# The order of the work at the start of a two-layer diffusion trunk: the second half of x loaded and normed before two of the four modulation chunks, more sums left open, and products of constants on TensorE

## The chip, the cores and the metric

The kernel runs on one core of a Trainium2 chip. The metric is device time in microseconds (us) of one execution, the median of three runs. 0.2% of it is 4.65 us.

TensorE (PE) multiplies into PSUM, which has eight banks; its weight loads (PEld) run beside its products. VectorE (DVE), ScalarE (ACT) and GpSimd (POOL) do the elementwise work, and SyncE's queue (SP) issues all transfers. Each engine takes its instructions in the order in which they stand, and waits on semaphores of the others.

## The reference, cut to what matters

Two layers, each for 128 context tokens and 512 latent tokens (640 in all, D = 1024). What the start of a layer computes:

```
mod = silu(cond) @ w_ada + b_ada
shift, scale, gate = split(mod, 3)
h = rms_norm(x, norm_g) * (1 + scale) + shift
z = h @ w_in
```

`cond` is one vector for the context tokens and one for the latents. After this come four mixers on parts of z (RWKV, latent attention, gMLP, FNet), gated merging, and x + gate * (merged @ w_out). The outputs are the normed x, the final RWKV states and the attention caches of the context.

## The kernel before, in words

All is kept with features on the partitions: x is 8 tiles of 128 features by 640 tokens, and the tokens are worked on in two halves of 320 (`HALVES`). A product of a float32 matrix with h is done as three products of rounded parts: a number is split into hi and lo (`split`, L143: hi on ScalarE, L144; lo on GpSimd, or on VectorE where the caller says V, L145), and `dense_half` (L161) adds hi*hi, hi*lo and lo*hi for each k of 8, lines 168 to 170, into one bank of PSUM. One column block of z for one half is thus 24 products of 320 columns.

The start of layer 0 stands in `layer` (L340), in the branch `l == 0`. Its parts, each a generator that can be run in steps:

- `load_x` (L304) issues 8 transfers of one half of x, 160 KB each.
- `norm_first` (L308): the squares on ScalarE and their sum on VectorE (L274, L276), `token_rstd` (L278) with two products with ones on PE (L280, L281), a reciprocal root with a Newton step (L186 to L193), then x times it, six tiles on VectorE and two on GpSimd (L316).
- `ada` (L236): the modulation in chunks of 512 outputs. Chunk 0 and 1 are the shift, 2 and 3 the scale; chunks 0 and 2 serve the features of k = 0 to 3, chunks 1 and 3 those of k = 4 to 7. They come in the order 0, 2, 1, 3. A chunk takes six steps: 4 transfers of 512 KB (`ar`); the products of its first four k; those of the other four (L249); the copy of the sum on ScalarE (L253); a step without work; four small products that turn the row into columns and add the bias (L258, L260).
- `tiles` (L319): `norm_scale` makes s = (1 + scale) * norm_g on VectorE (L291), and `norm_tile` (L294) makes h for one k: hi on ScalarE (L300), the same on VectorE (L301), and lo as the difference (L302), on VectorE for even k and on GpSimd for odd.
- `weights(i, k)` (L1187) loads and splits four k (256 KB) of the weights of column block 13 + i; `chunk(i, q)` (L1184) is that block for one half. Its four steps have two k each; the result is copied by ScalarE (L1185).

In the names of the profile, hhi and hlo are h's parts, wh and wl those of block 13, w10h to w30l those of blocks 14 to 16 for k = 0 to 3, and w14h to w34l for k = 4 to 7. m is a small sum in PSUM, dps a sum of `dense_half`.

Inside `tc.manual_schedule()` the instructions stand on each engine as the program is written; behind it a scheduler of the framework sets the order. Before the change: norm of the first half, chunk 0, weights, chunk 2, tiles 0 to 3 of the first half; then the four blocks' first parts (k = 0 to 3) are put between the steps of chunks 1 and 3, so that the blocks' sums stay open; then the weights of k = 4 to 7, x's second half is loaded, tiles 4 to 7 are made, and the open sums are finished while the second half is normed. Last, all four blocks of the second half.

PSUM is shared out by `banks` (L71): in this part four banks for sums of `dense_half` (`d`) and four for small sums (`m`, taken in turn by `bank1`, L78). The same place in layer 1 isn't touched.

Of the kernel before, what the change touches and what calls it, by code (L numbers as in the profile page):

```python
# [56 lines left out]
def trunk(ctx: ExitStack, tc: tile.TileContext, A: dict, O: dict, dbg: dict):  # L57
    nc = tc.nc
    mm = nc.tensor.matmul
# [280 lines left out]
    def layer(l, X, h, w13):  # L340
# [835 lines left out]
        with ExitStack() as es:  # L1176
# [4 lines left out]
            with tc.tile_pool(name=f"first{l}", bufs=1, side="right") as fp:  # L1181
# [14 lines left out]
                if l == 0:  # L1196


                    with tc.manual_schedule():
                        mod0 = ada(0, (0, 2, 1, 3), 8)  # L1200
                        w = [[], [], [], []]
                        run(norm_first(h, X, HALVES[0]))
                        run(steps(mod0, 6))
                        for i in range(3):
                            weights(i, 0, V)
                        run(steps(mod0, 6))
                        weights(3, 0)
                        weights(0, 4)
                        run(tiles(h, X, 0, HALVES[0]))
                        ahead = [chunk(i, HALVES[0]) for i in range(4)]  # L1210
                        run(steps(ahead[0], 2))
                        run(steps(mod0, 4))
                        run(steps(ahead[1], 2))
                        run(steps(mod0, 2))
                        run(steps(ahead[2], 2))
                        run(steps(mod0, 4))
                        run(steps(ahead[3], 1))
                        run(mod0)
                        run(steps(ahead[3], 1))
                        for i in range(1, 4):  # L1220
                            weights(i, 4)
                        load_x(X, HALVES[1])
                        nc.sync.dma_start(rope, A["rope"])
                        nc.sync.dma_start(fng, A["fng"])
                        run(tiles(h, X, 4, HALVES[0]))
                        second = seq(norm_first(h, X, HALVES[1]), tiles(h, X, 0, HALVES[1]), tiles(h, X, 4, HALVES[1]))
                        run(steps(second, 8))
                        run(ahead[0])
                        run(ahead[1])
                        mix(seq(*ahead[2:]), second, 4.0)  # L1230
                        run(second)
# [10 lines left out]
                for i in range(4):  # L1242
                    run(chunk(i, HALVES[1]))
# [131 lines left out]
    psum_l.enter_context(banks(4, 4))  # L1375
    X = new_x("x0")
# [171 lines left out]
```

## Time and profile before

| what | value |
|---|---|
| median of 3 runs | 2323.45 us (2320.99 to 2325.73) |
| profiled execution | 2330.01 us |
| span of its instructions | 2328.1 us |
| mean granted TensorE clock | 0.980 of 2.4 GHz |
| PE busy | 2183.5 us (94%) |
| DVE, ACT, POOL busy | 1449.2, 1098.4, 894.4 us |
| moved by DMA | 283.73 MB, mean 122 GB/s |

The span runs from the first to the last instruction; times in the rows are us from its start. Busy time is the union of an engine's instructions; products of PE overlap, so a busy PE need not be at its peak, and the granted clock (PEclk, 1.00 is 2.4 GHz, 0.50 is 1.2 GHz) stands beside it. In a row of a timeline, the bracket tells how long the engine was idle before the instruction, and whose work ended that. The change touches some 90 us at the start of the span; the first product of L199, at 88.64 us, comes behind it on PE.

### The profile page before, as it was taken

To read this page: it belongs to the slowest core of one execution; us is meant where nothing else is said; L and a number is where in the kernel's file an instruction comes from. 1 tells how busy PE (TensorE), PEld (TensorE's weight loads), DVE (VectorE), ACT (ScalarE), POOL (GpSimd) and SP (SyncE) were. 2 spreads that over 40 slices of the span, in tenths; PEclk is the share of its full clock that TensorE was granted. 3 is DMA by queue.
4 is the path that set the end of the run, shared out by engine and by line. 5 is a ranking of instruction groups with operands and counts; after the bars stand their busy time and mean duration, and the time that the engine had idled before them with its cause. 6 is when DMAs were issued, how large, how long until landed. Compare 5 with 4: busy or idle time off the path is not lost. (4 is left out here: it accounts for less than half of the span.)

```text
span 2328.1 us, 49632 instructions
## 1 busy us (share of the span) xinstructions
PE 2183.5 (94%) x19662; PEld 2013.7 (86%) x19662; DVE 1449.2 (62%) x2826; ACT 1098.4 (47%) x2387; POOL 894.4 (38%) x894
## 2 busy tenths in 40 slices
PE   6899998898999999899999999989999999998998
PEld 3788898787888999878998888978888899997997
DVE  4777757888884335822367787578889643367234
ACT  4566755444434334422355676544444343344332
POOL 2322224444433335523552212244444334355452
PEclk8999999999999999999999999999999999998999
DMA  7133336333215425565432323362332254264233
GB/s 262 51 108 95 93 98 194 101 100 100 85 56 177 143 80 179 155 219 203 151 98 87 105 81 99 115 197 86 99 88 70 62 178 152 76 187 147 91 102 106
DMA packets 208009, 283.73 MB, mean 122 GB/s; under 512 B 26912, under 2 KB 119712, under 8 KB 207776
## 3 DMA queue, kind: packets, MB, share of 16 engines
q1 hardware_dynamic: 207776, 280.55, 38.1%
q8 instruction: 155, 2.54, 0.5%
q14 instruction: 78, 0.64, 0.1%
HBM read 224.75 MB, written 55.74 MB: 120 GB/s over the span
## 5 line engine op out<-in xcount | busy, mean ns | idle before, releaser
L145 POOL TENSOR_TENSOR wl<-wr,wh 128x512 fp32r<-128x512 f32 x371 | 523.0, 1413 | 975.0 <-ACT wh L144 853.4
L168 PE MATMUL dps<-hhi,wh 128*128 128x320 f32 x2368 | 772.6, 326 | 10.8 <-DVE f L1146 4.2
L169 PE MATMUL dps<-hlo,wh 128*128 128x320 f32 x2368 | 744.7, 314 | 7.9 <-POOL hlo L302 4.5
L170 PE MATMUL dps<-hhi,wl 128*128 128x320 f32 x2368 | 742.2, 313 | 0.0
L168 PEld LDWEIGHTS dps<-hhi,wh 128*128 128x128 f32 x2368 | 452.7, 191 | 25.6 <-ACT hhi L300 4.8
L169 PEld LDWEIGHTS dps<-hlo,wh 128*128 128x128 f32 x2368 | 453.3, 191 | 14.6 <-POOL hlo L302 7.1
L170 PEld LDWEIGHTS dps<-hhi,wl 128*128 128x128 f32 x2368 | 452.1, 191 | 0.5
L144 ACT CAST wh<-wr 128x512 fp32r<-128x512 f32 x372 | 229.6, 620 | 311.0 <-PE dps L169 200.2
L168 PE MATMUL dps<-ohi,wh 128*128 128x320 f32 x512 | 161.6, 316 | 2.1 <-ACT wh L144 1.9
L170 PE MATMUL dps<-ohi,wl 128*128 128x320 f32 x512 | 158.7, 311 | 1.0 <-POOL wl L145 1.0
L822 DVE TENSOR_TENSOR XZ<-XZ,m 128x512 f16<-128x512 f16 x200 | 129.5, 677 | 47.4 <-PE m L819 47.3
L169 PE MATMUL dps<-olo,wh 128*128 128x320 f32 x512 | 159.0, 311 | 0.0
L1146 DVE SCALAR_TENSOR_TENSOR f<-f,dps 128x320 f32<-128x320 f32 x96 | 46.3, 486 | 169.3 <-PE dps L170 169.3
L769 POOL TENSOR_TENSOR GG<-GG,con 64x256 f32<-64x256 f32 x80 | 60.8, 760 | 163.8 <-DVE GG L764 160.6
L1140 ACT ACTIVATE f<-dps,der 128x320 f32<-128x320 f32 x128 | 67.2, 525 | 111.4 <-PE dps L170 104.1
L168 PEld LDWEIGHTS dps<-ohi,wh 128*128 128x128 f32 x512 | 97.0, 189 | 10.6 <-issue 5.9
L170 PEld LDWEIGHTS dps<-ohi,wl 128*128 128x128 f32 x512 | 96.6, 189 | 2.4 <-POOL wl L145 1.5
L169 PEld LDWEIGHTS dps<-olo,wh 128*128 128x128 f32 x512 | 96.9, 189 | 1.7 <-issue 1.7
L812 DVE TENSOR_TENSOR T<-m,con 128x256 f16<-128x256 f32 x200 | 80.7, 416 | 18.6 <-PE m L811 18.0
L774 ACT CAST A<-GG 64x256 f16<-64x256 f32 x80 | 32.3, 403 | 90.4 <-POOL GG L769 90.3
L615 DVE TENSOR_TENSOR pl<-m,ph 128x512 fp32r<-128x512 f32 (+1 forms) x96 | 59.1, 620 | 24.8 <-ACT ph L614 23.5
L818 PE MATMUL m<-T,XZ 128*128 128x64 f16 x800 | 66.0, 195 | 5.2 <-DVE T L812 5.2
(493 smaller groups left out, 4624.4 us busy)
## 6 DMA issues: line engine op xcount, KB each, us to landing
wr<-in_w_in SPq DMA_DIRECT2D x180, 256.0 KB, 2.9
wr<-in_w_merge SPq DMA_DIRECT2D x128, 256.0 KB, 2.7
ar<-in_w_ada SPq DMA_DIRECT2D x48, 512.0 KB, 6.3
wr<-in_w_branch SPq DMA_DIRECT2D x64, 256.0 KB, 2.8
zdr<-f SPq DMA_DIRECT2D x48, 320.0 KB, 3.4
rk<-spill SPq DMA_DIRECT2D x20, 768.0 KB, 5.9
thdr<-t SPq DMA_DIRECT2D x32, 320.0 KB, 3.2
odr<-t SPq DMA_DIRECT2D x32, 320.0 KB, 3.5
```

Of the source, the lines that this page charges most:

```text
L144: S_.copy(hi, src)
L145: (leng or G).tensor_sub(lo, src, hi.bitcast(F32))
L168: mm(ps, hi[:, c], ahi(k)[:, q], start=(k == 0), stop=False)
L169: mm(ps, hi[:, c], alo(k)[:, q], start=False, stop=False)
L170: mm(ps, lo[:, c], ahi(k)[:, q], start=False, stop=(k == K - 1))
L615: V.tensor_sub(pl[:, 0:w], tp[:, 0:w], ph[:, 0:w].bitcast(F32))
L769: G.tensor_sub(GK[HALF[j], j], GK[HALF[j], j], bc(i64[HALF[j]], 4))
L812: V.tensor_mul(T1.rearrange("p u (j k o i) -> p (u j) k o i", j=2, o=2, i=b)[:, :, :, 0, :], ps[:, 0:256].rearrange("p (x k i) -> p x k i" ...
L818: mm(ps[:, 64 * u:64 * u + 64], X1[:, u, :], cols(T1[:, u, :], 0), start=True, stop=True)
L822: V.tensor_add(new, new, ps.rearrange("p (x n i) -> p x n i", x=2, i=b))
L1140: yield from dense(A["w_merge"][l, m, n], 8, H, lambda q, ps: S_.activation(gt[:, q], ps, AF.Tanh, scale=0.5, bias=bias))
L1146: yield from dense(A["w_branch"][l, n, m], 4, (lambda k: o[k][0], lambda k: o[k][1]), lambda q, ps: V.scalar_tensor_tensor(to[:, q], gt[:, ...
```

## The change

- x's second half is loaded right behind the weights of k = 0 to 3, ahead of the transfers of chunks 1 and 3, and normed before the products of chunk 1.
- The four first parts of the first half follow one another without modulation between them. Then come the norm of the second half, chunk 1, tiles 0 to 3 of the second half, the first parts of blocks 13 and 14 for the second half (`late`), chunk 3, the weights of k = 4 to 7 (blocks 13 and 15 split on GpSimd, 14 and 16 on VectorE), tiles 4 to 7 of the first half, its four sums, tiles 4 to 7 of the second half, and the two late sums. Six sums are open at once, so `banks` gives six to `d` and two to `m`.
- `busy(n)` does n products of a 128x128 tile of ones with itself into a small bank, which nobody reads: 24 at the start, 4 in the middle of chunks 0 and 2, 8 behind each.
- Blocks 13 and 14 of the second half are no longer among the blocks behind the branch.

```diff
--- before.py
+++ after.py
@@ -1196,39 +1196,52 @@
                 if l == 0:
 
 
+                    def busy(n):
+
+                        ps = bank1()
+                        for _ in range(n):
+                            mm(ps[:, 0:128], ones, ones, start=True, stop=True)
+
                     with tc.manual_schedule():
                         mod0 = ada(0, (0, 2, 1, 3), 8)
                         w = [[], [], [], []]
+                        busy(24)
                         run(norm_first(h, X, HALVES[0]))
-                        run(steps(mod0, 6))
-                        for i in range(3):
-                            weights(i, 0, V)
-                        run(steps(mod0, 6))
-                        weights(3, 0)
-                        weights(0, 4)
+                        run(steps(mod0, 2))
+                        busy(4)
+                        run(steps(mod0, 4))
+                        weights(0, 0, V)
+                        busy(8)
+                        run(steps(mod0, 2))
+                        busy(4)
+                        run(steps(mod0, 4))
+                        busy(8)
+                        for i in range(1, 4):
+                            weights(i, 0, None if i == 3 else V)
+                        load_x(X, HALVES[1])
+                        run(steps(mod0, 1))
                         run(tiles(h, X, 0, HALVES[0]))
                         ahead = [chunk(i, HALVES[0]) for i in range(4)]
-                        run(steps(ahead[0], 2))
-                        run(steps(mod0, 4))
-                        run(steps(ahead[1], 2))
-                        run(steps(mod0, 2))
-                        run(steps(ahead[2], 2))
-                        run(steps(mod0, 4))
-                        run(steps(ahead[3], 1))
+                        for i in range(4):
+                            run(steps(ahead[i], 2))
+                        run(norm_first(h, X, HALVES[1]))
+                        run(steps(mod0, 5))
+                        run(steps(mod0, 1))
+                        run(tiles(h, X, 0, HALVES[1]))
+                        late = [chunk(i, HALVES[1]) for i in range(2)]
+                        for i in range(2):
+                            run(steps(late[i], 2))
                         run(mod0)
-                        run(steps(ahead[3], 1))
-                        for i in range(1, 4):
-                            weights(i, 4)
-                        load_x(X, HALVES[1])
+                        for i in range(4):
+                            weights(i, 4, V if i % 2 else None)
                         nc.sync.dma_start(rope, A["rope"])
                         nc.sync.dma_start(fng, A["fng"])
                         run(tiles(h, X, 4, HALVES[0]))
-                        second = seq(norm_first(h, X, HALVES[1]), tiles(h, X, 0, HALVES[1]), tiles(h, X, 4, HALVES[1]))
-                        run(steps(second, 8))
-                        run(ahead[0])
-                        run(ahead[1])
-                        mix(seq(*ahead[2:]), second, 4.0)
-                        run(second)
+                        for i in range(4):
+                            run(ahead[i])
+                        run(tiles(h, X, 4, HALVES[1]))
+                        for i in range(2):
+                            run(late[i])
                 else:
                     w = [w13, [], [], []]
                     second = norm_half(l, h, X, HALVES[1])
@@ -1239,7 +1252,7 @@
                         mix(chunk(i, HALVES[0]), second, 0.75 if i else 0.0)
                     run(second)
                 X["pool"].close()
-                for i in range(4):
+                for i in range(0 if l else 2, 4):
                     run(chunk(i, HALVES[1]))
                 shift(13, z, z13)
             rkv = proj_rkv(kp, z13)
@@ -1372,7 +1385,7 @@
 
 
     psum_l = ctx.enter_context(ExitStack())
-    psum_l.enter_context(banks(4, 4))
+    psum_l.enter_context(banks(6, 2))
     X = new_x("x0")
     h = new_h()
     pre = cst.tile([128, 1], F32, name="pre")
```

How this moves the instructions, at three places. SyncE's queue, from the chunk 0 transfers on; cond, x's first half and the constants stand ahead in both (ar is a piece of w_ada, wr a block of weights):

```order
 L244 DMA ar<-in_w_ada 128x1024 x4
-L149 DMA wr<-in_w_in 128x512 x3
+L149 DMA wr<-in_w_in 128x512
 L244 DMA ar<-in_w_ada 128x1024 x4
-L149 DMA wr<-in_w_in 128x512 x2
-L244 DMA ar<-in_w_ada 128x1024 x8
 L149 DMA wr<-in_w_in 128x512 x3
 L306 DMA x<-in_x 128x320 x8
-L1223 DMA rope<-in_rope 128x512
-L1224 DMA fng<-in_fng 128x8
+L244 DMA ar<-in_w_ada 128x1024 x8
+L149 DMA wr<-in_w_in 128x512 x4
```

One weight block instead of three stands ahead of chunk 2, and x's second half has passed the eight transfers of chunks 1 and 3.

VectorE, between the norm of x's first half and its first tile; before (the first mod is chunk 0, the second chunk 2):

```order
L260 TENSOR_TENSOR mod<-m_216,vec 128x8
L145 TENSOR_TENSOR wl<-wr,wh 128x512
L145 TENSOR_TENSOR w10l<-wr,w10h 128x512
L145 TENSOR_TENSOR w20l<-wr,w20h 128x512
L260 TENSOR_TENSOR mod<-m_259,vec 128x8
L291 SCALAR_TENSOR_TENSOR s_277<-mod,vec 128x8
L301 TENSOR_SCALAR t<-x,s_277,mod 128x128
```

and now:

```order
L260 TENSOR_TENSOR mod<-m_246,vec 128x8
L145 TENSOR_TENSOR wl<-wr,wh 128x512
L260 TENSOR_TENSOR mod<-m_291,vec 128x8
L145 TENSOR_TENSOR w10l<-wr,w10h 128x512
L145 TENSOR_TENSOR w20l<-wr,w20h 128x512
L291 SCALAR_TENSOR_TENSOR s_340<-mod,vec 128x8
L301 TENSOR_SCALAR t<-x,s_340,mod 128x128
```

The subtractions for w10l and w20l stood ahead of chunk 2's mod; now they stand between it and s, which every tile needs.

ScalarE, around the copy of chunk 3's sum (m_375 before, m_523 now); before:

```order
L253 COPY t<-m_324 128x512
L253 COPY t<-m_375 128x512
L144 CAST w14h<-wr 128x512
L144 CAST w24h<-wr 128x512
L144 CAST w34h<-wr 128x512
L300 ACTIVATE hhi<-x,mod,s_277 128x128
```

and now, where the first copy is chunk 1's and the four hhi are tiles 0 to 3 of the second half:

```order
L253 COPY t<-m_456 128x512
L300 ACTIVATE hhi<-x,mod,s_340 128x320 x4
L144 CAST uh<-ur 128x128
L253 COPY t<-m_523 128x512
L144 CAST wh<-wr 128x512
L144 CAST w14h<-wr 128x512
L144 CAST w24h<-wr 128x512
L144 CAST w34h<-wr 128x512
L144 CAST uh<-ur 128x128
L300 ACTIVATE hhi<-x,mod,s_340 128x128
```

Chunk 3's copy has four casts of weights behind it, where it had three (the fourth, wh, stood ahead of the first tile), and the tiles of the second half have moved ahead of it.

## Rows read from the trace of the kernel before

**Rows 1.** Stages: us; busy (x) of PE, PEld, DVE, ACT, POOL; PEclk, DMA share, GB/s

```profile
28.92:34.77 5.85, 4.59 (x12) 3.13 (x12) 3.75 (x10) 2.42 (x6) 1.90 (x3) 0.50 1.03 409
34.77:38.19 3.42, 3.42 (x17) 0.60 (x16) 0.00 (x0) 0.00 (x0) 0.00 (x0) 0.53 1.05 373
48.31:55.13 6.82, 3.79 (x13) 2.90 (x14) 6.39 (x13) 5.16 (x13) 3.24 (x4) 0.74 0.45 137
55.13:59.28 4.15, 4.15 (x19) 4.15 (x19) 1.67 (x4) 1.49 (x5) 0.00 (x0) 0.60 0.01 2
59.28:62.90 3.62, 3.62 (x24) 3.30 (x22) 1.74 (x5) 1.21 (x4) 1.76 (x2) 1.00 0.18 65
64.83:76.61 11.78, 8.07 (x38) 6.99 (x39) 9.68 (x16) 5.25 (x11) 8.80 (x8) 0.86 0.08 20
85.12:88.64 3.52, 3.52 (x26) 3.52 (x25) 1.31 (x3) 1.27 (x3) 0.00 (x0) 1.00 0.17 56
```

**Rows 2.** Waits of PE from 0 to 88.64: us in total, times, longest

```profile
PE dps L168 <- ACT hhi L300: 4.2, 3, 1.8
PE dps L169 <- POOL hlo L302: 3.3, 6, 1.2
PE dps L169 <- DVE hlo L302: 2.3, 2, 1.8
```

**Rows 3.** Timeline near 11 us: start, us, engine, line, operation, [idle before <-releaser]

```profile
10.28 1.27 PE L281 MATMUL m<-last,ones 128*128 128x320 f32 x2
...
11.42 0.20 DVE L1384 CAST c<-con 128x64 f16<-128x64 f32 x1 [2.49 <-DMA con<-in_consts]
...
12.26 0.49 DVE L283 TENSOR_SCALAR t<-m 128x320 f32<-128x320 f32 x1
```

**Rows 4.** Timeline from 21 to 30 us

```profile
21.31 0.69 DVE L145 TENSOR_TENSOR w20l<-wr,w20h 128x512 fp32r<-128x512 f32 x1
...
27.37 0.54 DVE L291 SCALAR_TENSOR_TENSOR s<-mod,vec 128x8 f32<-128x8 f32 x1
...
28.92 0.63 PE L168 MATMUL dps<-hhi,wh 128*128 128x320 f32 x1 [1.79 <-ACT hhi L300]
29.58 0.49 DVE L302 TENSOR_TENSOR hlo<-t,hhi 128x320 fp32r<-128x320 f32 x1
```

**Rows 5.** Timeline of PE, first and last product of w14 and of w34

```profile
55.13 0.47 PE L168 MATMUL dps<-hhi,w14h 128*128 128x320 f32 x1
...
58.06 0.47 PE L170 MATMUL dps<-hhi,w14l 128*128 128x320 f32 x1
...
61.24 0.31 PE L168 MATMUL dps<-hhi,w34h 128*128 128x320 f32 x1
...
62.86 0.31 PE L170 MATMUL dps<-hhi,w34l 128*128 128x320 f32 x1
```

**Rows 6.** Timeline of PE, VectorE and GpSimd, norm and tiles of the second half

```profile
59.28 0.70 PE L280 MATMUL m<-acc,ones 128*128 128x320 f32 x2
...
64.83 0.41 PE L168 MATMUL dps<-hhi,wh 128*128 128x320 f32 x1 [1.66 <-ACT hhi L300]
...
70.68 0.97 DVE L302 TENSOR_TENSOR hlo<-t,hhi 128x320 fp32r<-128x320 f32 x1
...
70.36 0.94 POOL L302 TENSOR_TENSOR hlo<-t,hhi 128x320 fp32r<-128x320 f32 x1 [0.85 <-DVE t L301]
```

**Rows 7.** Timeline from 42 to 47 us, chunk 3 of the modulation

```profile
42.82 1.92 PE L249 MATMUL m<-ar,cond 128*32 128x512 f32 x16
...
45.29 0.62 ACT L144 CAST w14h<-wr 128x512 fp32r<-128x512 f32 x1
...
45.81 0.62 ACT L144 CAST w24h<-wr 128x512 fp32r<-128x512 f32 x1
...
46.64 0.17 DVE L260 TENSOR_TENSOR mod<-m,vec 128x8 f32<-128x8 f32 x1 [5.42 <-PE m L258]
...
46.84 0.45 DVE L291 SCALAR_TENSOR_TENSOR s<-mod,vec 128x8 f32<-128x8 f32 x1
```

## The prediction

> **What bounds the kernel now.** The change touches only the start of layer 0, so I read the start. First the table by stage [rows 1]: look at PE's busy time beside the length of the stretch, and at PEclk. From the first product on the normalised x (28.92) to the first product of line 199 (88.64), behind which the order of the work is the same in both kernels, PE has three stretches of work that comes in drops: 28.92 to 34.77, 48.31 to 55.13 and 64.83 to 76.61, in which 12, 13 and 38 products fill 5.85, 6.82 and 11.78 us. Between them are stretches where PE is busy all the time, some at a granted clock of 0.50 to 0.60 of 2.4 GHz. Then the waits of PE in this time [rows 2]: 4.2 us for ScalarE's hhi, 3.3 and 2.3 us for hlo from GpSimd and VectorE. So the norm tiles bound the drops, not the transfers. Ahead of 28.92 PE has only the modulation and the norm's two products to do.
>
> How fast PE can be: twelve products of 320 columns stand 1.62 us from first to last start at full clock (61.24 to 62.86), 2.93 us at half (55.13 to 58.06) [rows 5]. That is 0.147 and 0.266 us each; 12 cost 1.8 or 3.2 us.
>
> **What costs nothing.** The 48 products of 128x128 constants have no row. The nearest are the 128x320 float32 products of L280 and L281, 0.70 us at 59.28 and 1.27 us at 10.28 [rows 3, 6]; by columns 0.28 to 0.51 us each. The first 24 take 6.7 to 12.2 us and may hold L281 back from 10.28 until 13; VectorE then first waits for con until 11.42 and starts L283 at 12.26 [rows 3], and x is wanted only at the first tile, near 28. The groups of four and eight lie between pieces of w_ada that come at 373 GB/s or a little more [rows 1], 1.4 us for 512 KB, and beside ScalarE's and VectorE's steps on the sums; only the last eight can matter (below). With two m banks each new sum waits for the reader of the one but last, long done. Six d banks hold four ahead and two late sums, so no product waits for a bank. On SP's queue, x's second half passes the eight pieces of chunks 1 and 3: 1.3 MB at 409 GB/s [rows 1] puts them back 3.2 us, but they are used only after 41 and 55; the k = 4 weights behind them come near 42 and are used near 58.
>
> **The walk through the new order**, against the same mark at 88.64:
>
> 1. First product. Two weight blocks fewer, 0.52 MB at 0.40 MB/us, stand ahead of chunk 2, so it ends 1.3 us sooner. But on VectorE s (L291) now stands behind w10l and w20l, whose blocks come after chunk 2: 2.0 us for three blocks, then casts 0.5 apart [rows 7] and a subtraction of 0.69 [rows 4]. That puts s near 27.3 as before (27.37), and the product at 28.92 [rows 4]. I take 28.9; ends: 1.3 us sooner, or 1.0 later if the last eight products of constants (8 x 0.51 = 4.1 us, from near 25.8, where chunk 2's small products should end) run at half clock.
> 2. The first four tiles take the 5.85 us of before [rows 1]: to 34.8. At full clock 0.5 less.
> 3. Chunks 1 to 3 now follow at once: 36 products. In this place before, the clock was 0.50 to 0.53 until 38.2 [rows 1]. I take 12 at half clock and 24 at full: 3.2 + 3.5 = 6.7, to 41.5; ends 5.3 and 9.6.
> 4. L280 of the second half stands behind those 36. From L280 to the first product on that half it took 59.28 to 64.83, 5.55 us [rows 6]: to 47.0. Chunk 1's modulation lies inside it (1.92 [rows 7] and its two small steps). No other product is left for PE there.
> 5. Four tiles of the second half: the fourth tile's hlo was done at 71.30 [rows 6], 6.5 us after 64.83; with its two products 7.0, then chunk 1's twelve, 1.8: to 55.8. Ends -1.5 and +1.4.
> 6. Chunk 3 comes only now. 1.92 for its products, then 1.90 to mod (44.74 to 46.64), as before [rows 7]: 59.6. On ScalarE the four casts of the k = 4 weights wait behind the copy of this sum; they end 4 x 0.52 after it, near 60.5; VectorE subtracts w14l and w34l ahead of s. w34l ends near 61.3, and from s to the first product is 1.47 us (46.84 to 48.31 [rows 7, 1]). To 63.0. Before, this link took 48.31 - 44.74 = 3.6 us, now 5.3. Ends -0.7 and +1.9 (chunk 3 at half clock, 3.42 us [rows 1], and the two subtractions beside GpSimd's).
> 7. Tiles 4 to 7 of the first half: 5.85, to 68.9 (6.8 before, when GpSimd still worked on weights; that is the upper end).
> 8. 36 products: 5.3 at full clock, 9.6 at half. I take 5.9, to 74.8.
> 9. The rest: 72 products of the second half, 10.6, and 24 of the next chunk, 3.52 [rows 1]. ScalarE's hhi for tiles 4 to 7 stand behind the copies of the four finished sums, so they start near 75; chunk 2's products run meanwhile and cover most. I take 1.5 us of waiting (0 to 4): 90.4.
>
> So the mark goes from 88.64 to 90.4, **1.8 us later**: the interleaving that is given up (modulation between the open sums) is worth about what x's earlier half brings. The profiled execution took 2330.0 (span 2328.1), so it would take 2331.8; the median shown is 6.6 us below it, which gives 2325.2. I say 2325.
>
> [...] The row: VectorE's hlo took 0.97 us beside GpSimd's 0.94, and 0.49 alone [rows 6, 4], so it is slowed by about the overlap. [...]
>
> **The rivals.** A change within 0.2% of 2323.45 (4.65 us, 2318.8 to 2328.1) is what a measurement of this kernel can't tell from none.
>
> *Faster: every step at its lower end.* The mechanism is the clock: the products of constants hold 2.4 GHz from the start, PE comes out of the first tiles at full clock, L280 is reached sooner, and everything behind it moves up. Steps 1 to 9 then give -1.3, -0.5, -1.4, 0, -1.5, -0.7, 0, -0.6, -1.5: 7.5 us below my sum, 2317.7. For it: the stretch of 34.77 to 38.19 lost half its rate to a clock that fell while PE had little to do [rows 1]. Against it: the new products end near 28, and drops of work that a tile at a time feeds come right after. [...] I give 0.17.
>
> *Slower: the clock falls at the new waits.* Steps 4 to 6 hold 21.5 us with 24 products and two modulation chunks, steps 7 and 9 more drops. In 48.31 to 59.28 a clock that fell among tiles stayed at 0.60 through a busy stretch of 4.15 us [rows 1]. If PE enters step 8 at half clock (+3.7), runs step 5's last twelve so (+1.4) and chunk 3 (+1.5), the mark is 6.6 us later than my sum: 2331.8. It decides at the granted clock near 69. 0.23.
>
> *The change doesn't do what it says.* The products of constants end, the clock is back at 1.2 GHz at the first tile, chunk 2 waits for nothing less: then steps 1 and 3 are at their upper ends (+1.0, +2.9) and the rest as walked, 5.7 us later than before, or 2329 at the worst, while a part of it only gives 2325 to 2328. I count its worst with the slower case.
>
> **How the numbers follow.** My sum and what lies within 4.65 us of before: 0.60. Faster 0.17, slower 0.23. The range 2317.5 to 2331.5 runs from the faster rival to the slower one and leaves out the tails, some 0.2.
>
> **What would show it.** Right: first product on x near 29; no modulation products between it and 41; L280 a second time near 40 to 42; first product on the second half near 45 to 47; chunk 3's products near 54 to 56, and hhi of k = 4 only near 61 to 63, behind w34l; L199 near 90. PE then waits for hhi and hlo about as long as before, in four places instead of three. Wrong: PEclk 1.00 without a gap from 10 to 60 and L199 before 85 (the faster rival), or PEclk 0.5 near 60 to 75 and L199 behind 94 (the slower one), or a wait of PE for DMA in this stretch, which I have at nothing.

## The result, and the profile after

The change is slower. The changed kernel took 2339.56 us (median of 6, 2333.43 to 2340.68), the kernel before, beside it, 2324.59 (2320.99 to 2328.51): ratio 1.006, 95% interval 1.0045 to 1.0074. Two more comparisons gave 1.0047 (1.0034 to 1.0059) and 1.0045 (1.0029 to 1.0061). So it costs 10 to 14 us. I had said 2325.0, between 2317.5 and 2331.5, and had given slower a chance of 0.23.

The profiled execution took 2340.68 us, its span 2337.9, 9.8 more than the span before. The mark, the first product of L199, stands at 93.92 instead of 88.64: 5.3 of the 9.8 arise ahead of it, 4.5 behind it. Stages of the changed kernel up to the mark, cut as steps 2 to 9 of the prediction were (columns as in [rows 1]):

```profile
30.51:35.67 5.16, 3.36 (x13) 2.25 (x13) 4.85 (x11) 4.94 (x13) 1.84 (x2) 0.81 0.97 392
35.67:43.16 7.49, 7.49 (x37) 7.49 (x37) 1.67 (x4) 0.47 (x2) 0.00 (x0) 0.67 0.84 313
43.16:48.34 5.18, 4.15 (x30) 1.96 (x28) 3.20 (x6) 1.71 (x3) 1.13 (x2) 1.00 0.01 3
48.34:55.92 7.58, 4.04 (x13) 3.22 (x14) 6.73 (x18) 1.93 (x4) 3.32 (x4) 0.66 0.00 0
55.92:58.54 2.62, 2.62 (x13) 2.43 (x12) 0.00 (x0) 0.00 (x0) 0.00 (x0) 0.67 0.09 25
58.54:66.61 8.07, 2.98 (x26) 1.39 (x25) 3.93 (x7) 3.85 (x9) 3.79 (x3) 0.87 0.26 89
66.61:71.72 5.11, 4.35 (x12) 3.31 (x13) 3.54 (x9) 3.44 (x8) 2.55 (x3) 0.50 0.23 79
71.72:78.35 6.63, 6.63 (x38) 6.63 (x38) 0.00 (x0) 1.28 (x3) 1.72 (x2) 0.78 0.27 80
78.35:93.92 15.57, 14.87 (x98) 14.09 (x97) 9.21 (x13) 8.98 (x17) 3.41 (x5) 1.00 0.10 32
```

The three places where PE gets its work in drops are still there (first, fourth and seventh row), as in [rows 1]. But the 36 products that follow at once (second row) take 7.49 us at a mean granted clock of 0.67. PE's waits up to the mark:

```profile
PE dps L168 <- ACT hhi L300: 6.3, 3, 4.3
PE dps L169 <- POOL hlo L302: 3.4, 7, 0.8
PE dps L169 <- DVE hlo L302: 3.3, 1, 3.3
...
PE m L249 <- DMA ar<-in_w_ada: 2.2, 1, 2.2
```

The wait for hhi has grown from 4.2 us to 6.3 [rows 2], by the one of 4.3 behind chunk 3, and that for VectorE's hlo from 2.3 to 3.3; that for GpSimd's hlo is as long as before. PE waits for a transfer for 2.2 us only, once, ahead of chunk 0's products (12.64).

The first product on x, at 30.51 instead of 28.92 [rows 4], is 1.6 us later than I said. The timeline from 19.9 us on (each product of constants leaves two records, so 48 are x96 in all):

```profile
19.98 2.03 PE L1203 MATMUL m<-ones 128*128 128x128 f32 x16
...
21.94 1.07 PE L249 MATMUL m<-ar,cond 128*32 128x512 f32 x8
...
22.93 1.16 PE L1203 MATMUL m<-ones 128*128 128x128 f32 x8
...
24.02 1.07 PE L249 MATMUL m<-ar,cond 128*32 128x512 f32 x8
...
26.79 2.03 PE L1203 MATMUL m<-ones 128*128 128x128 f32 x16
26.97 0.17 DVE L260 TENSOR_TENSOR mod<-m,vec 128x8 f32<-128x8 f32 x1 [6.04 <-PE m L258]
...
29.34 0.15 DVE L291 SCALAR_TENSOR_TENSOR s<-mod,vec 128x8 f32<-128x8 f32 x1
...
30.51 0.41 PE L168 MATMUL dps<-hhi,wh 128*128 128x320 f32 x1 [1.69 <-ACT hhi L300]
```

Chunk 2's products (21.94, 24.02) stand behind eight and then four products of constants. The kernel with the new order and none of these (order_only, below) shows that their data was there earlier:

```profile
19.87 1.95 PE L249 MATMUL m<-ar,cond 128*32 128x512 f32 x12
...
22.07 1.05 PE L249 MATMUL m<-ar,cond 128*32 128x512 f32 x4 [0.25 <-DMA ar<-in_w_ada]
...
24.95 0.17 DVE L260 TENSOR_TENSOR mod<-m,vec 128x8 f32<-128x8 f32 x1 [4.20 <-PE m L258]
...
27.32 0.15 DVE L291 SCALAR_TENSOR_TENSOR s<-mod,vec 128x8 f32<-128x8 f32 x1
...
28.49 0.63 PE L168 MATMUL dps<-hhi,wh 128*128 128x320 f32 x1 [3.58 <-ACT hhi L300]
```

There chunk 2's first products start at 19.87, its mod stands at 24.95 instead of 26.97, and the first product at 28.49. In both, s stands 2.37 us behind mod. So the products of constants hold chunk 2, and with it everything up to the first tile, back by 2.0 us.

### The profile page after: what moved, and what is told of

It reads as the page before. It is cut to its first block, busy times and chain, and to the rows that moved or that the text cites. A ratio compares the mean times of both kernels' runs of the same rounds, so it can differ in the third digit from the quotient of the medians.

```text
span 2337.9 us, 49827 instructions
## 1 busy us (share of the span) xinstructions
PE 2196.8 (94%) x19758; PEld 2031.1 (87%) x19758; DVE 1451.3 (62%) x2828; ACT 1099.3 (47%) x2387; POOL 892.7 (38%) x892
## 5 line engine op out<-in xcount | busy, mean ns | idle before, releaser
L145 POOL TENSOR_TENSOR wl<-wr,wh 128x512 fp32r<-128x512 f32 x371 | 524.3, 1417 | 976.5 <-ACT wh L144 864.1
L168 PEld LDWEIGHTS dps<-ohi,wh 128*128 128x128 f32 x512 | 97.4, 190 | 11.6 <-issue 5.9
```

Of the source, the lines that this page charges most:

```text
L145: (leng or G).tensor_sub(lo, src, hi.bitcast(F32))
L168: mm(ps, hi[:, c], ahi(k)[:, q], start=(k == 0), stop=False)
```

## The experiments

The mark is read from each kernel's one trace; "behind" is its span less the mark. Ratios are against the kernel before, run on the same chip in the same session. The row before2, the kernel before against itself, shows that ratios are good to some 0.1%. The traced execution can lie at either end of a kernel's runs (after3's took 2333.46 us, its median is 2338.71; order_pool1's 2324.60, median 2329.42; hold_only's 2340.00, median 2335.29), so the two right columns are those of one execution each.

| kernel | ratio (95%) | mark | behind |
|---|---|---|---|
| before (first trace) | 1 | 88.6 | 2239.5 |
| before2 | 0.9991 (0.9982 to 1.0000) | 89.2 | 2240.9 |
| after (first trace) | 1.0060 (1.0045 to 1.0074) | 93.9 | 2244.0 |
| after2 | 1.0047 (1.0034 to 1.0059) | 93.8 | 2247.5 |
| after3 | 1.0045 (1.0029 to 1.0061) | 91.0 | 2240.4 |
| busy_only | 1.0008 (0.9997 to 1.0019) | 87.2 | 2244.8 |
| before_busy32 | 1.0009 (1.0000 to 1.0019) | 87.0 | 2238.3 |
| order_only | 1.0023 (1.0014 to 1.0033) | 89.0 | 2244.5 |
| order_pool1 | 1.0010 (1.0000 to 1.0019) | 89.3 | 2233.5 |
| order_w | 1.0016 (1.0007 to 1.0024) | 88.8 | 2245.6 |
| before_pool_1 | 1.0016 (1.0008 to 1.0025) | 88.6 | 2240.5 |
| after_pool1 | 1.0047 (1.0032 to 1.0062) | 92.0 | 2244.7 |
| after_pool1b | 1.0037 (1.0023 to 1.0052) | 93.0 | 2243.6 |
| after_first | 1.0023 (1.0013 to 1.0033) | 90.7 | 2239.3 |
| first_pool1 | 1.0013 (1.0004 to 1.0023) | 91.3 | 2239.5 |
| after_nohold | 1.0033 (1.0022 to 1.0044) | 90.7 | 2241.2 |
| hold_only | 1.0037 (1.0025 to 1.0049) | 91.3 | 2246.9 |
| last8_only | 1.0018 (1.0009 to 1.0027) | 90.0 | 2236.7 |
| pre8h | 1.0020 (1.0011 to 1.0029) | 92.3 | 2237.3 |
| pre4 | 1.0009 (1.0000 to 1.0019) | 88.9 | 2237.1 |

**The two kernels again, and each part alone.** before2 and after2 are unchanged. busy_only is before with the 48 products of constants; order_only is the change without them:

```diff
 busy_only, against before
+                        busy(24)
                         run(norm_first(h, X, HALVES[0]))
-                        run(steps(mod0, 6))
+                        run(steps(mod0, 2))
+                        busy(4)
+                        run(steps(mod0, 4))
...
+                        busy(8)
...
```

> The kernel before, unchanged, for a second trace. Two theories on the 9.8 us between the two profiled spans, of which 5.3 stand at the first product of line 199 (93.9 against 88.6) and the rest behind it. Theory 1, place: what is lost is lost ahead of line 199, and behind it the half-clock stretches fall by chance. Then the half-clock stretches behind 100 us stand elsewhere here than in the first trace, the mark is within 2 us of 88.6, and the span behind the mark differs from the first trace's 2239.5 us by several us. Theory 2, behind: the later part is lost by a cause that each execution repeats. Then the span behind the mark is 2239.5 within 1.5 us and the half-clock stretches stand in the same places.

> The changed kernel, unchanged, for a second trace. Theory 1, place: the mark is near 94 again and the span behind it is as long as in either trace of before, within the few us by which those two differ. Theory 2, behind: the span behind the mark is 4 us or more longer than in both traces of before, with additional half-clock stretches near 468, 1178 and 1908 us as in the first trace. Time about 2340 by both.

> Before with only the 48 products of constants, at the same places in the modulation. If the products of constants cost the time (they hold back the sums, or push the half-clock stretches to worse places): 5 us or more above before, mark at 92 or later. If the order costs it: within 3 us of before, mark 86 to 90. If they do what they are for, PE comes out of the first tiles at full clock and the mark is 1 to 3 us earlier than 88.6.

> The change without the 48 products of constants: the new order and six open sums alone. If the order costs the time: 12 to 18 us above before, mark 92 to 97. If the products of constants cost it: within 4 us of before, mark near 90 as my walk had it.

The repeated traces show both kinds of loss. The mark of before is 89.2 again and that of after 93.8; behind it, the two of after are 2244.0 and 2247.5 us long, the two of before 2239.5 and 2240.9. The additional half-clock stretches (granted clock 0.50) that the expectation of after2 puts near 468, 1178 and 1908 begin at 457.0, 1167.0 and 1897.4 in the first trace; after2 has the first two of them, after3 (below) only the first. Neither part alone moves the mark back much: the order has it at 89.0, the products of constants in the old order at 87.2. Together they have it at 93.9 and 93.8, and at 91.0 in after3. Rows of order_only tell a part of why (stages as above, its tiles, its 36 products, chunk 1's twelve, and the 36 of k = 4 to 7):

```profile
28.49:33.66 5.17, 4.36 (x13) 3.32 (x14) 4.86 (x11) 4.94 (x13) 1.85 (x2) 0.50 1.02 417
33.66:39.58 5.92, 5.92 (x37) 5.92 (x37) 1.67 (x4) 0.47 (x2) 0.00 (x0) 0.88 1.03 393
...
52.25:54.10 1.85, 1.85 (x14) 1.66 (x12) 0.00 (x0) 0.00 (x0) 0.00 (x0) 1.00 0.12 35
...
67.30:73.44 6.14, 6.14 (x38) 6.14 (x37) 0.00 (x0) 1.28 (x3) 1.70 (x2) 0.85 0.32 89
```

Without the products of constants the clock is at 0.50 while tiles feed PE, which costs little, and up for most of the 36 products (5.92 us at 0.88). In the first trace of after it is up for most of the tiles (0.81), which gain nothing (5.16 against 5.17 us), and falls in the 36 products (7.49 at 0.67). The twelve (2.62 against 1.85) and the later 36 (6.63 against 6.14) lose to the clock too. But this differs between executions, and a lift through the tiles is not what it takes. Tiles and 36 products in after3, and in first_pool1, which has only the first 24 products of constants (below):

```profile
30.61:35.47 4.86, 2.93 (x13) 1.96 (x14) 4.55 (x11) 4.64 (x13) 1.83 (x2) 1.00 1.02 411
35.47:40.76 5.29, 5.29 (x39) 5.29 (x38) 1.96 (x4) 0.77 (x3) 0.00 (x0) 1.00 1.03 388
```

```profile
28.91:34.07 5.16, 4.35 (x12) 3.31 (x13) 4.85 (x11) 4.93 (x13) 1.84 (x2) 0.50 0.99 381
34.07:40.98 6.91, 6.91 (x37) 6.91 (x37) 1.68 (x4) 0.48 (x2) 0.00 (x0) 0.74 1.01 394
```

In after3 both ran at full clock, and its mark is 91.0. In first_pool1 the tiles ran at 0.50, as in order_only, and the 36 products still lost 1.0 us against it. In all 13 traces with the new order the four tiles took 4.86 to 5.17 us, whatever the clock. The 36 products took 5.9 to 6.2 us in the three kernels without products of constants, where the clock was up again at 35.1 to 35.4 us, and 6.4 to 7.5 in every trace with some of them but after3's; in these nine it was up again at 36.2 to 40.6. So the products of constants go with a half-clock stretch that reaches further into the 36 products. What sets its place in one execution is not shown.

And order_only, with the mark of before, is still 0.23% slower: it loses behind the mark.

**Where it is lost behind the mark.** How much later, in us, the same instruction of ScalarE starts than in the first trace of before, near some points of that trace:

| near | 150 | 440 | 480 | 960 | 1180 | 1980 | 2110 | end |
|---|---|---|---|---|---|---|---|---|
| before2 | 0.5 | 0.6 | 0.6 | 0.1 | 5.1 | 3.3 | 2.4 | 2.0 |
| order_only | 0.8 | 0.2 | 2.2 | 1.7 | 4.0 | 3.9 | 4.0 | 5.4 |
| after | 5.7 | 6.1 | 8.1 | 10.0 | 11.6 | 9.8 | 9.7 | 9.8 |
| after2 | 5.6 | 6.4 | 8.4 | 11.6 | 14.3 | 11.4 | 13.5 | 13.2 |
| after3 | 2.8 | 5.9 | 7.9 | 5.0 | 7.2 | 2.4 | 3.9 | 3.3 |
| before_pool_1 | 0.3 | 0.0 | 1.9 | 1.3 | 4.0 | 2.2 | 2.0 | 1.0 |
| after_pool1 | 3.4 | 3.3 | 3.4 | 5.1 | 7.8 | 7.6 | 7.3 | 8.5 |
| order_pool1 | 0.7 | 0.3 | 0.4 | 1.2 | 2.3 | -3.7 | -4.2 | -5.3 |
| hold_only | 2.8 | 2.1 | 2.2 | 5.4 | 8.2 | 4.7 | 9.6 | 10.1 |

The distance doesn't drift, it jumps up or down by 1 to 3 us at some ten places, most of them half-clock stretches that one trace has and another doesn't. Many jumps differ between two traces of one kernel. One doesn't: the 2.0 us between 440 and 480, which order_only and all traces of the changed kernel have, and no trace of before. GpSimd and VectorE there, in before:

```profile
446.68 0.10 POOL L731 MEMSET P<- 128x4 f32 x1
...
446.89 0.41 DVE L752 SCALAR_TENSOR_TENSOR Qs<-rk,P 128x256 f32<-128x256 f32 x1
...
447.08 1.36 POOL L145 TENSOR_TENSOR wl<-wr,wh 128x512 fp32r<-128x512 f32 x1 [0.30 <-ACT ZZ L848]
...
449.24 0.22 PE L827 MATMUL m<-XZ,A 64*64 64x64 f16 x2 [1.20 <-DVE XZ L822]
```

and in order_only:

```profile
446.94 0.10 POOL L731 MEMSET P<- 128x4 f32 x1
...
447.06 1.32 POOL L145 TENSOR_TENSOR wl<-wr,wh 128x512 fp32r<-128x512 f32 x1
...
447.15 1.51 DVE L752 SCALAR_TENSOR_TENSOR Qs<-rk,P 128x256 f32<-128x256 f32 x1
...
449.99 0.22 PE L827 MATMUL m<-XZ,A 64*64 64x64 f16 x2 [1.69 <-DVE XZ L822]
```

In before, GpSimd sits idle for 0.30 us ahead of a subtraction (L145). The bracket names ScalarE's ZZ, but the subtraction doesn't need it: in order_only it starts at 447.06 and ZZ ends at 447.09. There it starts 0.02 us behind the instruction before it, and VectorE's Qs, 0.09 us later, takes 1.51 us instead of 0.41, to 0.28 us behind GpSimd's end. PE then waits 1.69 us instead of 1.20, and a half-clock stretch follows (451.5).

The order behind the mark is the same; what differs is the length of what stands ahead. GpSimd's program has 1663 instructions in the trace of before, its waits for semaphores included, and 1662 with the new order. So I tried moving that place by one instruction and nothing else, back in the change and away in before:

```diff
 after_pool1, against after
     G.memset(smask, 1.0)
+    G.memset(smask, 1.0)

 before_pool_1, against before
-    G.memset(cond32, 0.0)
+    V.memset(cond32, 0.0)
```

> The changed kernel with one more instruction on GpSimd at its start (smask is set to 1.0 twice). In six traces, the three with before's GpSimd program have 0.30 us of unexplained idle time ahead of one weight subtraction (L145, 447.08 us in before) and VectorE's Qs at 446.89 takes 0.41 us; the three with the new order, whose GpSimd program is one instruction shorter, have 0.01 us there, the subtraction starts earlier, Qs takes 1.50 us, and a half-clock stretch follows near 457. Theory 1, place in the program: GpSimd stalls about 0.3 us at fixed instruction numbers, 128 apart. Then the 0.30 us are back here, Qs takes 0.41, no half-clock stretch near 457, and the time is 1 to 2.5 us below the changed kernel's. Theory 2, timing: the difference comes from where transfers and products stand in the new order. Then 0.01 and 1.50 stay, and the time is the changed kernel's within 1 us. The mark (first product of line 199) 93.9 by both.

> The kernel before with one instruction less on GpSimd: cond32 is set to zero by VectorE. Theory 1, place in the program: the subtraction of 447 us starts without the 0.30 us, VectorE's Qs takes 1.5 us, a half-clock stretch may follow near 451, and the time is 0.5 to 2.5 us above before; the mark stays at 88.6 to 89.2. Theory 2, timing: 0.30 and 0.41 stay, no change.

In the traces theory 1 holds in both directions. before_pool_1, which does the same work at the same mark:

```profile
446.76 1.32 POOL L145 TENSOR_TENSOR wl<-wr,wh 128x512 fp32r<-128x512 f32 x1
...
446.85 1.51 DVE L752 SCALAR_TENSOR_TENSOR Qs<-rk,P 128x256 f32<-128x256 f32 x1
```

after_pool1 (its lines are numbered one higher):

```profile
450.24 0.41 DVE L753 SCALAR_TENSOR_TENSOR Qs<-rk,P 128x256 f32<-128x256 f32 x1
...
450.44 1.36 POOL L146 TENSOR_TENSOR wl<-wr,wh 128x512 fp32r<-128x512 f32 x1 [0.30 <-ACT ZZ L849]
```

before_pool_1 jumps by 1.9 us between 440 and 480 and after_pool1 by 0.1, and before_pool_1 is 0.16% slower for one memset that changed its engine (VectorE's program has 3401 instructions in both traces, one memset more and one wait less, so later places on VectorE don't move). But after_pool1 was no faster than the changed kernel, as far as two sessions can be compared; so both ran again side by side, and order_only got the same instruction:

```diff
 order_pool1 against order_only, after_pool1b against after3
     G.memset(smask, 1.0)
+    G.memset(smask, 1.0)
```

> The new order without the products of constants, with one more instruction on GpSimd at its start. Without it this order took 1.0023 of before, with the mark at 89.0 as in before. Theory 1, GpSimd's place: taking one GpSimd instruction out of before cost 0.16% with the mark unmoved, so putting it back here gives 3 to 4 us: time within 2 us of before, 0.30 us idle ahead of the subtraction near 447, Qs 0.41. Theory 2, any shift: before stands well in the half-clock stretches behind the mark, and any other arrangement of the engines' instructions costs 3 to 6 us there. Then the 0.30 and 0.41 come back, but the time stays 3 to 6 us above before.

> The changed kernel once more, for times on one chip with the next three. 1.0045 to 1.006 of before; first product 30.5, mark 92 to 94.

> The changed kernel with one more GpSimd instruction, again. Theory 1, GpSimd's place: 2 to 4 us below the changed kernel on the same chip. Theory 2, any shift: the same within 1.5 us.

All three traces with the instruction have the 0.30 and the 0.41 us back. The gain is 1.0045 to 1.0037 in the change and 1.0023 to 1.0010 in order_only: 2 to 3 us, the size of the jump, though the intervals overlap. So the place is settled by the traces; its worth by the times only roughly. The half-clock stretch behind it stands in all six traces in which GpSimd's program is one shorter (after, after2, after3, order_only, before_pool_1, after_first), and in one of the fourteen others: before_busy32 (below) has the 0.30 and the 0.41 us and still a clock of 0.50 from 448.7 on, and loses 1.4 us between 440 and 480. The stall's place makes the stretch likely, but the stretch can come without it.

**Which products of constants.** after_first keeps the first 24 alone, first_pool1 is the same with the GpSimd instruction. The three after it have that instruction too: after_nohold lacks only the 8 and 4 that stand ahead of chunk 2's products, hold_only has the 24 and those 12, last8_only the last 8 alone.

```diff
 after_nohold, against after_pool1
                         weights(0, 0, V)
-                        busy(8)
                         run(steps(mod0, 2))
-                        busy(4)
                         run(steps(mod0, 4))
                         busy(8)

 after_first, against after
-                        busy(4)
...
-                        busy(8)
...
-                        busy(4)
...
-                        busy(8)
```

> The changed kernel with only the first 24 products of constants; the 4, 8, 4 and 8 between the chunks of the modulation are left out. Theory 1: those 24 stand ahead of chunk 2's products on TensorE (16 from 19.98 on, 8 at 22.93) and hold chunk 2 back by 2.0 us, and they move the half-clock stretch out of the first tiles into the 36 products behind (7.5 us instead of 5.9). Then the first product is near 28.5, the 36 products take 6 us, and the mark is 89 to 90, as without any. Theory 2: the first 24 do it. Then first product 30.5 and mark 94.

> The changed kernel with only the first 24 products of constants and one more GpSimd instruction. If the two causes make up the whole: mark 89 to 91, time 0 to 3 us above before. If the place of GpSimd's instructions does not matter here: 4 to 6 above, as with the first 24 alone.

> The changed kernel without just the 8 and 4 products of constants that stand ahead of and within chunk 2 on TensorE (36 of 48 stay), and with one more GpSimd instruction. If those 12 hold chunk 2 back: first product 28.3 to 29.2 instead of 30.5, mark 89 to 91.5, time 5 us or more below the changed kernel and 1 to 4 above before. If the last 8 do it: first product 30 or later, mark 92 or later.

> The changed kernel with the first 24 products of constants and the 8 and 4 that hold chunk 2 back, without the 4 in chunk 0 and the last 8; one more GpSimd instruction. Theory 1, holding chunk 2 back costs: first product 30.5, mark 92 to 94, time 6 to 9 us above before. Theory 2, the last 8 cost, by where the clock falls: first product 30.5, but tiles at half clock and the 36 products behind at full, and the time 3 to 5 us above before.

> The new order with only the last 8 products of constants, behind chunk 2; one more GpSimd instruction. Without any products of constants this was 1.0010 of before (2.7 us). Theory 1, these 8 lie in idle time and cost nothing: first product 28.3 to 28.6, 2 to 4 us above before. Theory 2, they keep the clock up through the first tiles, it falls in the 36 products behind, and in some executions that costs: 5 to 7 us above before, runs further apart than before's (over 8 us).

The 24 later ones cost the time: with the first 24 alone the first product is at 28.7 and the kernel at 1.0023, or 1.0013 with the GpSimd instruction, as without any (1.0010). From after_pool1b to first_pool1 that is 0.24%, 5.6 us, with intervals that only touch. The first 24 alone do put the mark back, by some 2 us (90.7 and 91.3 against 89.0 and 89.3), but that doesn't show in the time. Of the later ones, the 12 hold chunk 2 back, as expected: without them (after_nohold) the first product is at 28.48, in the six traces with them at 29.48 to 31.56. But the times don't add up by groups. hold_only is as slow as after_pool1b, the last 8 alone cost some 0.08%, within the noise, and yet taking the 12 away gives back only 0.04%, 1 us, where I expected 5 or more. One more place has a part in it. Between 1980 and 2110 hold_only loses 4.9 us and after_nohold 3.2, hold_only without any half-clock stretch between 2035 and 2121. There ScalarE waits for loads of o (waits in us, times, longest); before:

```profile
ACT ohi L144 <- DMA olo<-odr: 3.4, 2, 2.4
```

hold_only:

```profile
ACT ohi L145 <- DMA olo<-odr: 8.9, 4, 3.5
```

In after_nohold it is idle for 8.6 us ahead of these casts, in every other kernel for 5.2 at most. These two alone have 36 products of constants. Why the loads come later wasn't tried and stays open, and with it why the later products of constants cost more than the mark shows.

**A delay alone.** Loads of x's second half, loaded again later, ahead of all others:

```diff
 pre8h, against before
+    for k in range(8):
+        nc.sync.dma_start(X["x"][:, k, 320:480], A["x"][k][:, 320:480])
     load_x(X, HALVES[0])

 pre4, against before
+    for k in range(4):
+        nc.sync.dma_start(X["x"][:, k, HALVES[1]], A["x"][k][:, HALVES[1]])
     load_x(X, HALVES[0])
```

> [...] Theory 1: what is lost or won behind the mark by where the half-clock stretches fall is chance, and before stands well in it. Then the mark is 1.6 us later, but the time rises by 3 to 7 us. Theory 2: behind the mark nothing depends on it. Then the time rises by 1.6, within 1 us.

> The kernel before with four loads of 164 KB (x's second half, loaded again later) ahead of everything on SP's queue. [...] Theory 1, places: a delay passes through as it is, since no engine's program changes its length: time +1.5 to +3 us. [...]

In before's first trace the half-clock stretches are 3.41, 6.83 or 10.24 us long, one to three steps of 3.41 (27.74 to 37.98, for one), save the one that runs to the end of the trace. I was wrong on the size of the delay: with eight small loads the mark came 3.7 us later (0.46 for each); with four of whole halves the first product came 1.2 us later, at 30.07, but the mark only 0.3. The times rose by 0.20% and 0.09%, 4.6 and 2 us: about what the delay adds. So the idea that any shift in time costs 3 to 6 us behind the mark is not borne out by these two, while one GpSimd instruction less cost some 4 us (1.9 to 5.8) without any delay.

**Two tries for something better.** before_busy32 has 32 products of constants ahead of the first sum in before's order. order_w is order_only with the weights of k = 4 to 7 ahead of chunk 3, and four more memsets on GpSimd:

```diff
 before_busy32, against before
                         w = [[], [], [], []]
+                        busy(32)
                         run(norm_first(h, X, HALVES[0]))

 order_w, against order_only
+                        for i in range(4):
+                            weights(i, 4, V if i % 2 else None)
                         run(mod0)
-                        for i in range(4):
-                            weights(i, 4, V if i % 2 else None)
     G.memset(smask, 1.0)
+    G.memset(smask, 1.0)
...
```

> The kernel before with 32 products of constants ahead of the first sum and none later (with 48 spread over the modulation the mark came 1.5 us earlier, the time 0.08% later). Theory 1: what the 48 cost behind the mark hangs on where TensorE's instructions stand, and 32 keep that to within a full 128 of them: the mark 0.5 to 2 us earlier than 88.9, the time 0 to 2 us below before. Theory 2, any shift: time 1 to 5 us above before.

> The new order without the products of constants, with the casts and subtractions of the k = 4 weights put ahead of chunk 3's products instead of behind (and GpSimd's program kept at before's length by four memsets). If step 6 is what those two subtractions and four casts make it (5.4 us from chunk 3's small products to the first product of tiles 4 to 7, 56.79 to 62.17): that link takes 3.4 to 4.0 us and the mark is 1.4 to 2.2 us earlier than 89.0. If chunk 3 and its chain bound it anyway: within 0.7 us of 89.0. Time by theory 1 (places and mark): 1 to 2 us below before; by theory 2 (any shift): 2 to 4 above.

before_busy32 has the earliest mark of all, 87.0, and isn't faster for it: 1.0009. So its theory 1, that the constants' cost behind the mark comes from where TensorE's later instructions stand, isn't borne out either; nothing else tests it. order_w shortens the link behind chunk 3, but chunk 3 starts at 55.96 instead of 54.10, and the mark is 88.84. Of these 1.9 us, 1.3 are the twelve products ahead of it (3.15 us at a granted clock of 0.54, against 1.85 at 1.00), 0.4 the tiles ahead of those, and 0.3 a later first product. No kernel here beats before.

## Why the prediction was wrong

By its steps, in the changed kernel's first trace, and in order_only's:

| step | said | after | order_only |
|---|---|---|---|
| 1 first product | 28.9 | 30.5 | 28.5 |
| 2 first four tiles | 5.85 | 5.16 | 5.17 |
| 3 36 products | 6.7 | 7.49 | 5.92 |
| 4 norm of the second half | 5.55 | 5.18 | 5.18 |
| 5 four tiles and twelve products | 8.8 | 10.2 | 9.34 |
| 6 chunk 3 to the next tile | 7.2 | 8.07 | 8.07 |
| 7 tiles 4 to 7 | 5.85 | 5.11 | 5.13 |
| 8 36 products | 5.9 | 6.63 | 6.14 |
| 9 the rest | 15.6 | 15.57 | 15.59 |
| mark | 90.4 | 93.9 | 89.0 |

**The walk through the order held up, in part by luck.** No single step is off by more than 0.9 us in order_only, but five are too long by 0.4 to 0.8 and three too short, so that the errors cancel in part: its mark is 89.0, where before's is and 1.4 us ahead of my 90.4. With GpSimd's place restored, the order alone costs 0.10%, about what I gave the whole change.

**The step that failed first is "What costs nothing".** I put the groups of four and eight "between pieces of w_ada" and let only the last eight matter. They stood in front of pieces that had already landed, and held chunk 2 back by 2.0 us, where the upper end of step 1 allowed 1.0, and that for the last eight, which alone held nothing back (last8_only, 28.47). They were even cheaper than I had them: eight took 2.03 us, 0.25 each, against my 0.28 to 0.51. And I saw a faster clock only as a gain; the one way in which I let the products of constants fail was that they end and the clock is at half again at the first tile. In after it was still up at the first tile, and fell at 33.7, so that the 36 products of step 3 lost what the tiles could not use. All in all the 24 later products of constants cost some 5 us (after_pool1b against first_pool1). The hold and the clock are seen in the traces; that they make up these 5 us is not shown, since the groups don't add up.

**The second is the sentence that behind L199 "the order of the work is the same in both kernels".** The order is the same, and I took it that the time must be. 4.5 us of the first 9.8 arose there. About 2 of them are GpSimd's place at 447, shown in the traces by moving it both ways. The rest, half-clock stretches that come and go and the loads near 2050, differs between traces of one kernel, and what of it the change causes stays open.

**Step 6 was too short by what I left out.** I took 7.2 us from chunk 3 to the next tile, with VectorE's last subtraction ahead of s about as long as one alone, 0.69 us [rows 4]. It was 8.07:

```profile
58.54 1.92 PE L249 MATMUL m<-ar,cond 128*32 128x512 f32 x16
...
62.32 0.17 DVE L260 TENSOR_TENSOR mod<-m,vec 128x8 f32<-128x8 f32 x1 [7.04 <-PE m L258]
62.40 1.18 DVE L145 TENSOR_TENSOR w14l<-wr,w14h 128x512 fp32r<-128x512 f32 x1
...
62.99 1.71 POOL L145 TENSOR_TENSOR w24l<-wr,w24h 128x512 fp32r<-128x512 f32 x1
...
63.51 1.74 DVE L145 TENSOR_TENSOR w34l<-wr,w34h 128x512 fp32r<-128x512 f32 x1
...
65.17 0.41 DVE L291 SCALAR_TENSOR_TENSOR s<-mod,vec 128x8 f32<-128x8 f32 x1
...
66.61 0.63 PE L168 MATMUL dps<-hhi,wh 128*128 128x320 f32 x1 [4.33 <-ACT hhi L300]
```

VectorE's two subtractions take 1.18 and 1.74 us beside GpSimd's of 1.71, against 0.69 for one alone [rows 4]. So s stands 2.85 us behind mod. I had seen VectorE's hlo take 0.97 us beside GpSimd's and 0.49 alone [rows 6, 4], but let such a loss into the upper end of step 6 only (+1.9); the row asked for a part of it in the sum. With the subtractions moved away (order_w) the same link is

```profile
59.73 0.17 DVE L264 TENSOR_TENSOR mod<-m,vec 128x8 f32<-128x8 f32 x1 [7.13 <-PE m L262]
59.93 0.53 DVE L295 SCALAR_TENSOR_TENSOR s<-mod,vec 128x8 f32<-128x8 f32 x1
...
61.48 0.42 PE L172 MATMUL dps<-hhi,wh 128*128 128x320 f32 x1 [1.79 <-ACT hhi L304]
```

0.2 us from mod to s, and 5.5 us for the whole.

**The rivals.** The slower one named the right direction for the wrong place, and its 2331.8 is still short of what came: the clock near 69 was down in after and in order_only alike (0.50), and didn't decide. Step 9 came out as said (15.57 and 15.59 us against 15.6). PE's waits for hhi and hlo did not stay "about as long as before": in after they are 13.0 us in all, against 9.8 [rows 2].

## What to carry to other kernels

Filler work for TensorE must not stand ahead of real work whose inputs have landed (here it held chunk 2 back by 2.0 us), and a faster clock in a stretch that waits on other engines gained little (the four tiles took 5.17 us at 0.50 in order_only, 5.16 at 0.81 in after, 4.86 at 1.00 in after3): look where the clock falls afterwards, in more than one trace. Where a change leaves later code as it was, don't price that code at nothing: with one instruction more or less on GpSimd or ScalarE, idle times of 0.27 to 0.30 us came ahead of other instructions, and on GpSimd this was worth 2 to 3 us here, more than the 1.8 us that I had forecast for the whole change. So test an edit of a few us beside a neutral variant, such as one with a memset more, before calling it good or bad.

## What the runs showed of the hardware that I had not expected

- **GpSimd and ScalarE stalled at fixed places of their programs.** In before against order_only, whose ScalarE program is one instruction longer and GpSimd's one shorter, idle times of 0.27 to 0.30 us move to the neighbouring instruction. On GpSimd they stand at 286 and 447 us in before, 128 instructions apart, waits counted; on ScalarE at 330, 517, 712, 831 and 1192 us, 256, 256, 128 and 384 instructions apart, all whole multiples of 128. The page of the changed kernel counts transfers of instructions (transfers, MB, share of 16 engines):

```profile
q8 instruction: 155, 2.54, 0.4%
q14 instruction: 78, 0.64, 0.1%
```

The second queue moved 8.2 KB each time, the first 16.4. Its 78 transfers fit 128 instructions each, by my estimate: the four engines other than TensorE have 9950 in this trace, and 9950 / 128 is 77.7. In the trace of before a transfer of the second queue starts 0.6 to 1.3 us behind the end of each of the seven idle times named (at 287.0, 331.4, 447.7, 517.7, 712.8, 831.8 and 1192.5). That the engines wait for such transfers is my estimate from this and from the two counts of 128, and is not shown. That the stalls go by instruction number is shown for GpSimd by after_pool1 (0.30 us idle at 450.44) and before_pool_1 (none at 446.76). The step between two stalls is 128 in two cases, and 0.3 us were enough to turn who came first at 447.
- **0.3 us became 2.** The stall in before is lucky: it lets VectorE's Qs go ahead of GpSimd's subtraction. Without it Qs takes 1.1 us longer (1.51 against 0.41), PE waits 0.5 longer (1.69 against 1.20), and in all six such traces the granted clock falls to 0.50 for a stretch; between 440 and 480 this comes to 2.0 us in order_only and 1.9 in before_pool_1.
